# Gates and z: one 512-column matmul over high and low rows, halves added at eviction

## The chip, the cores and the metric

One core of one Trainium2 chip. The metric is the device time of one execution in microseconds (us), lowest is best; times of several runs are given as a median. A profile is one execution taken by the hardware profiler; its times count from its first instruction.

## The reference

Two layers over 256 latent tokens and 256 context tokens, 2048 channels, all in float32. Layer 0 projects the modulated, normalised tokens `h` by one weight `w_in` (2048 x 14400) into q, a gate, z, k, v, the X, B and C inputs of a state-space scan (SSD), and dt. Neighbourhood attention (16 heads of 128) is multiplied with the silu of the gate, the scan's output with the silu of z; both together go through `w_out`. Layer 1 is a gated short convolution.

```python
p = h @ w_in
...
ya = neighbourhood_attention(q, k, v, kc, vc, rpb).reshape(b, seq, NA_WIDTH)
ya = ya * jax.nn.silu(cols(p, COL_GATE_A, NA_WIDTH, 0))
...
yb = gated_group_rmsnorm(y_ssd + d * lat[0], cols(p, COL_Z, SSD_WIDTH, 0), ssm_norm_g)
out = jnp.concatenate([ya, yb], axis=-1) @ w_out
```

The gate, z, q and C are needed for the 256 latent tokens alone; k, v, X and B for latent and context tokens.

## The kernel before

**Precision.** Each float32 operand is split into a high part in the fast matmul format (`F32R`, a copy on ScalarE, called ACT) and a low part, the rest (a subtraction on VectorE, called DVE). A product is three matmuls into one PSUM bank: high by high, high by low, low by high. `hH[kb]` and `hL[kb]` (kb 0 to 15) are the split rows of block kb of the 2048 input channels, 512 columns each: 256 latent and 256 context tokens.

**Weights.** Loads of 512 KB (1024 elements on each of 128 partitions) come through the queue on SyncE in a written order (`q_proj`, `weight`), into five buffers `raw`; ACT writes the high half (L422) and DVE the low half (L429) into one of three places `w`. A load of a 512-column projection holds 2 row blocks in rows of 2 KB, one of a 256-column projection 4 row blocks in rows of 1 KB. Places used by the gate, z and C weights are shifted by 16 elements (`shifted`).

**Projections.** `proj(columns, kind, banks, ...)` walks the 16 row blocks and calls `chunk`, which takes the next split weight and issues matmuls (all recorded at L196). Kind "act" keeps the rows in the array and streams 512 weight columns (`mm_act`, for q, k, v). Kind 512 or 256 keeps a weight block of 128 columns in the array and streams 512 or 256 token columns (`mm_ws`): 512 for B and X, 256 for C, the gate and z. With 256, two weight blocks share a bank, 256 columns each, and three matmuls of 256 columns are issued for each weight block and row block.

**Order.** For group a (or s) 0 to 3, `do_qk`, `do_g` (gate, 512 columns), the values, and `do_ssd` (B, C, X in 4 banks, z with 512 columns) follow each other. Between the matmuls, `pump` lets generators issue their work: evictions (`urgent`), attention heads and scan groups (`side`), and dot products of the modulation for later (`back`). A planner keeps a time for each engine and each buffer and lets a task issue when its operands are due; `banks(n)` issues other work until n of the 8 PSUM banks are free; `reserve` keeps banks from side tasks toward the end of a projection.

**Eviction of gate and z** (`silu2_gen`): for each of the two banks of a unit, ACT takes a tanh of 512 columns (L1125) into a temporary, and DVE multiplies (th + 1) with the bank into `gt` or `sz` (L1127). It waits until the previous group is done with `gt` or `sz`, and until K of group 0 is done, since partial sums of K lie in those two buffers at the start.

**Tiles.** `xnT[kb]`, the transposed normalised rows, lie in the tiles of `hL` (blocks 0 and 1 in `Bl`, `Cl`) until block kb is modulated and split in `ada_gen`. Later the split mixer outputs (`mix`), the rows of layer 1 (`h1`) and its outputs (`y2`) take the places of `hH` and `hL`.

Of the kernel before, what the change touches and what calls it, by code (L numbers as in the profile page):

```python
# [9 lines left out]
F32R = mybir.dt.float32r  # L10
AF = mybir.ActivationFunctionType
ALU = mybir.AluOpType
# [129 lines left out]
def kernel(ctx: ExitStack, tc, x, cx, ada0, w0, adaT, w_in, w_out, sc_in, sc_out, rpb, small, const,  # L142
# [406 lines left out]
    for j in range(1, 8):  # L549
# [8 lines left out]
        if j < 7:  # L558
# [6 lines left out]
    order = list(range(0, 6)) + list(range(8, 16)) + [6, 7]  # L565
    ssd_cols = lambda s: [(w_in, COL_B + s * 256, 256), (w_in, COL_C + s * 256, 256), (w_in, COL_X + s * 512, 512),
                          (w_in, COL_Z + s * 512, 512)]
    q_proj(w_in, CG(0), 512)
# [4 lines left out]
    for a in range(1, 4):  # L573
        qk = [(w_in, CQ(a), 512), (w_in, CK(a), 512)]
        gv = [(w_in, CG(a), 512), (w_in, CV(a), 512)][::-1 if a in () else 1]
        for j_ in qk + gv + ssd_cols(a) if a < 3 else qk + ssd_cols(a) + gv:
            q_proj(*j_)
# [33 lines left out]
    xnT = [st([128, 512], ("Bl", "Cl")[kb] if kb < 2 else f"hL{kb}", name=f"xm{kb}") for kb in range(KB)]  # L611
# [51 lines left out]
    hH, hL = [None] * KB, [None] * KB  # L663

# [10 lines left out]
    def mm_ws(ps, actH, actL, H, Lo, n, first, last):  # L675

        for b in range(H.shape[-1] // 128):
            bb = slice(b * 128, (b + 1) * 128)
            if n == 512:
                o, f = ps[b], first  # L680
            else:
                o, f = ps[b // 2][:, (b % 2) * 256:(b % 2) * 256 + 256], first and b % 2 == 0
            mm(o, H[:, bb], actH[:, :n], f, False)
            mm(o, H[:, bb], actL[:, :n], False, False)
            mm(o, Lo[:, bb], actH[:, :n], False, last)
            if n == 512 or b % 2:
                pump()

    def chunk(kb0, kind, ps, first, last, lhs=None):
# [3 lines left out]
        for j in range(nb):  # L693
# [3 lines left out]
            if kind == "act":  # L697
                mm_act(ps, aH, aL, H[:, j], Lo[:, j], f, l)
            else:
                mm_ws(ps, aH, aL, H[:, j], Lo[:, j], kind, f, l)  # L700
# [21 lines left out]
    def ada_gen():  # L722
        bc = lambda ap: ap.unsqueeze(2).to_broadcast([128, 2, 2])
        for j in range(8):
# [39 lines left out]
            for ts in ((0, 1), (2,), (3,)) if j == 0 else ((0, 1, 2, 3),):  # L764
# [4 lines left out]
                for kb in (2 * j, 2 * j + 1):  # L769
# [5 lines left out]
                    if hH[kb] is None:  # L775
                        hH[kb] = st([128, 512], f"hH{kb}", F32R, name=f"hH{kb}")
# [13 lines left out]
                    if hL[kb] is None:  # L790
                        hL[kb] = st([128, 512], f"hL{kb}", F32R, name=f"hL{kb}")
# [213 lines left out]
    def put_mix(i, o):  # L1005
        if free_rows[0] > i % 16:

            yield W_("ACT", o)
            hl = st([128, 2, 256], f"hH{i}" if i < 16 else f"hL{i - 16}", F32R, name=f"mix{i}")
# [110 lines left out]
    def silu2_gen(key, a, ps, dst, ok):  # L1120
        yield when(lambda: ok())
        for b in range(2):
            yield W_("ACT", ps[b])
            th = tmp()
            E(S.activation(th, ps[b], AF.Tanh, scale=0.5))  # L1125
            yield W_("DVE", th)
# [1094 lines left out]
```

## Time and profile before

| | |
|---|---|
| median of 3 runs | 1740.03 us (1739.43 to 1740.67) |
| profiled execution, first to last instruction | 1738.3 us |
| TensorE (PE) busy | 1717.7 us, 99%, 9255 matmuls |
| weight loads (PEld) | 1451.5 us, 84% |
| VectorE (DVE) busy | 1253.3 us, 72% |
| ScalarE (ACT) busy | 776.2 us, 45% |
| memory read and written | 224 GB/s over the span |

The profiled execution has no time of its own beside its span; the median of the runs is 1.7 us over that span. Busy time of matmuls is modelled and overlaps from one to the next, so the distance between the starts of matmuls is what one takes in a stream. A row of the timeline is: start, length, engine, line and operation, output and inputs, shape, and how many instructions in a row were merged (x2). A row of a group is: line, engine, operation, output and inputs, shape, count, busy us, mean ns of one, and the idle time of the engine before them.

### The profile page before, as it was taken

Reading aid. Unit: us, or ns where it says so; the run is one execution under the profiler, and the core shown is the slowest. Engines: PE = TensorE matmul, PEld = TensorE weight load, DVE = VectorE, ACT = ScalarE, POOL = GpSimd, SP = SyncE. Lnnn points to the kernel's source line nnn. Section 1 sums busy time; section 2 is a strip of 40 time slices with the busy share of each in tenths; the row PEclk is TensorE's granted clock in tenths of the full one; section 3 lists DMA queues with packets and bytes.
Section 4 is the critical chain, followed back from the end, with each engine's and each line's share of the span. In section 5 each row is a group of like instructions: output and inputs, shape, how many; then the busy total and the mean of one; then the engine's idle time right before and its main releaser. Section 6 shows DMA issues by size and latency. Waiting matters only on the chain.

```text
span 1738.3 us, 24820 instructions
## 1 busy us (share of the span) xinstructions
PE 1717.7 (99%) x9255; PEld 1451.5 (84%) x9255; DVE 1253.3 (72%) x2108; ACT 776.2 (45%) x1367; POOL 33.2 (2%) x28
## 2 busy tenths in 40 slices
PE   6999999999999999999999999999999999999999
PEld 4777989889888889888888898888888888888887
DVE  5698787877576877676877687887668667665654
ACT  6434544445243445243435243665445344444442
POOL 0000100001000001000000000000000000000000
PEclk9999999999999999999999999999999999999999
DMA  9987644566754765755766567767867888776763
GB/s 375 366 319 271 206 135 142 180 209 187 228 183 151 234 210 183 227 188 164 230 221 195 191 196 248 258 225 254 280 204 260 267 272 284 246 241 191 248 213 114
DMA packets 192391, 391.03 MB, mean 225 GB/s; under 512 B 16200, under 2 KB 45960, under 8 KB 192016
## 3 DMA queue, kind: packets, MB, share of 16 engines
q1 hardware_dynamic: 184960, 382.88, 67.8%
q10 hardware_dynamic: 7312, 6.59, 1.2%
q8 instruction: 72, 1.18, 0.3%
q14 instruction: 47, 0.39, 0.1%
HBM read 379.79 MB, written 9.62 MB: 224 GB/s over the span
## 4 chain that ended last, share of the span: by engine, by line
PE 96%; DMA 2%; DVE 2%; issue 0%; SPq 0%; ACT 0%; POOL 0%; DVEq 0%; ACTq 0%
PE bank L196 93%; PE bank L200 3%; DMA raw<-in_ada 1%; DMA full<-dram_crow 1%; DVE csb L859 0%; DVE w L429 0%; DVE raw L859 0%; SPq L603 0%; DVE gt L818 0%; DVE yi L859 0%; DVE tmp L623 0%; DVE hL L792 0%; DVE sz L818 0%; DVE tmp L2116 0%; SPq L383 0%
## 5 line engine op out<-in xcount | busy, mean ns | idle before, releaser
L422 ACT CAST w<-raw 128x1024 fp32r<-128x1024 f32 (+1 forms) x344 | 359.8, 1047 | 554.7 <-PE bank L196 462.0
L429 DVE TENSOR_TENSOR w<-raw,w 128x1024 fp32r<-128x1024 f32 (+1 forms) x344 | 417.2, 1216 | 239.5 <-ACT w L422 238.2
L196 PE MATMUL bank<-hH,w 128*128 128x256 f32 (+1 forms) x2064 | 487.0, 325 | 0.0
L196 PE MATMUL bank<-w,hH 128*128 128x512 f32 x1280 | 405.7, 396 | 4.0 <-ACT hH L780 2.5
L196 PEld LDWEIGHTS bank<-hH,w 128*128 128x128 f32 x2064 | 345.3, 188 | 32.1 <-issue 1.7
L196 PE MATMUL bank<-hL,w 128*128 128x256 f32 (+1 forms) x1040 | 335.0, 322 | 0.0
L196 PEld LDWEIGHTS bank<-w,hH 128*128 128x128 f32 x1280 | 237.1, 188 | 56.3 <-DVE gt L818 3.4
L196 PE MATMUL bank<-w,hL 128*128 128x512 f32 x640 | 250.0, 391 | 0.2
L196 PEld LDWEIGHTS bank<-hL,w 128*128 128x128 f32 x1040 | 196.5, 189 | 14.5
L196 PE MATMUL bank<-w,h 128*128 128x512 f32 x768 | 178.2, 390 | 0.0
L196 PEld LDWEIGHTS bank<-w,h 128*128 128x128 f32 x768 | 144.1, 188 | 29.7
L888 DVE CUSTOM_DVE_ANT_0 raw<-raw,csb 128x1024 f32<-128x1024 f32 x128 | 155.3, 1218 | 11.9 <-DMA raw<-in_adaT 9.1
L196 PEld LDWEIGHTS bank<-w,hL 128*128 128x128 f32 x640 | 120.2, 188 | 25.7 <-DVE hL L792 0.9
L196 PE MATMUL bank<-w,mix 128*128 128x512 f32 x588 | 137.8, 391 | 0.0
L196 PEld LDWEIGHTS bank<-w,mix 128*128 128x128 f32 x588 | 109.7, 188 | 22.2 <-issue 0.3
L1371 DVE SCALAR_TENSOR_TENSOR tmp<-bank,cwh,tmp 128x508 f32<-128x508 f32 (+1 forms) x96 | 71.3, 746 | 1.9
L196 PE MATMUL bank<-KL,h 128*128 128x512 f32 x264 | 63.9, 390 | 0.0
L196 PEld LDWEIGHTS bank<-KL,h 128*128 128x128 f32 x264 | 49.5, 188 | 10.2
L196 PE MATMUL bank<-wH,h 128*128 128x512 f32 x168 | 55.7, 391 | 0.0
L196 PE MATMUL bank<-QT,h 128*128 128x512 f32 x168 | 55.7, 391 | 0.0
L429 DVE TENSOR_TENSOR wL<-raw,wH 128x1024 fp32r<-128x1024 f32 x31 | 37.9, 1223 | 23.9 <-ACT wH L422 23.8
L429 DVE TENSOR_TENSOR QL<-raw,QT 128x1024 fp32r<-128x1024 f32 x32 | 39.1, 1223 | 22.1 <-ACT QT L422 21.8
(306 smaller groups left out, 1962.3 us busy)
## 6 DMA issues: line engine op xcount, KB each, us to landing
raw<-in_w_in SPq DMA_DIRECT2D x196, 512.0 KB, 3.8
raw<-in_adaT SPq DMA_DIRECT2D x128, 512.0 KB, 4.8
raw<-in_sc_in SPq DMA_DIRECT2D x128, 512.0 KB, 4.7
raw<-in_w_out SPq DMA_DIRECT2D x64, 512.0 KB, 4.5
raw<-in_ada SPq DMA_DIRECT2D x35, 512.0 KB, 7.7
raw<-in_sc_out SPq DMA_DIRECT2D x32, 512.0 KB, 4.7
raw<-in_w SPq DMA_DIRECT2D x16, 512.0 KB, 5.5
tmp<-dram_csr SPq DMA_DIRECT2D x32, 256.0 KB, 5.2
```

What stands on the lines that cost most here:

```text
L196: E(T.matmul(o, l, r, start=start, stop=stop, skip_group_check=True))
L200: E(T.transpose(o, i, ident if k == 128 else ident[:k, :k]))
L422: E(S.copy(H, v))
L429: E(V.tensor_tensor(out=Lo, in0=v, in1=H.bitcast(F32), op=ALU.subtract))
L888: E(V.tensor_tensor_reduce(out=raw, in0=raw, in1=csb, scale=1.0, scalar=0.0, op0=ALU.mult, op1=ALU.add, accum_out=gp[:, h, m:m + 1]))
L1371: E(V.scalar_tensor_tensor(out=do, in0=di, scalar=cwh[:, 32 * k + ch:32 * k + ch + 1], in1=do, op0=ALU.mult, op1=ALU.add))
```

## The change

The 512 gate or z columns of a group are projected in two halves of 256 (two weight blocks each), with a bank for each weight block. For a weight block and a row block, one matmul of the high weights streams the 256 high and the 256 low latent columns side by side (512 columns, into the two halves of the bank), and a second streams the 256 high columns against the low weights into the first half. At the eviction ACT copies the bank's second half into `gt` or `sz`, DVE adds the first half to it, and, when both blocks of the half are there, tanh and the multiply follow from and to that buffer. The rows' high and low parts become one tile `hh[kb]` of two times 512 columns, so that one access pattern reaches both; the normalised rows of the start lie in the tiles of later odd blocks and in `Bl`, `Cl`. C keeps its three matmuls of 256 columns (`mm_quarter`). The weights of gate and z are loaded as 256-column projections.

```diff
@@ -563,16 +563,18 @@
...
     order = list(range(0, 6)) + list(range(8, 16)) + [6, 7]
+    halves = lambda c0: [(w_in, c0, 256), (w_in, c0 + 256, 256)]
     ssd_cols = lambda s: [(w_in, COL_B + s * 256, 256), (w_in, COL_C + s * 256, 256), (w_in, COL_X + s * 512, 512),
-                          (w_in, COL_Z + s * 512, 512)]
-    q_proj(w_in, CG(0), 512)
+                          *halves(COL_Z + s * 512)]
+    for j_ in halves(CG(0)):
+        q_proj(*j_)
     for r0 in (0, 1024):
...
         qk = [(w_in, CQ(a), 512), (w_in, CK(a), 512)]
-        gv = [(w_in, CG(a), 512), (w_in, CV(a), 512)][::-1 if a in () else 1]
+        gv = halves(CG(a)) + [(w_in, CV(a), 512)]
         for j_ in qk + gv + ssd_cols(a) if a < 3 else qk + ssd_cols(a) + gv:
@@ -608,7 +610,12 @@
...
     E(V.tensor_scalar(out=bs1, in0=P_("ab0")[:, 16:32], scalar1=1.0, scalar2=None, op0=ALU.add))
-    xnT = [st([128, 512], ("Bl", "Cl")[kb] if kb < 2 else f"hL{kb}", name=f"xm{kb}") for kb in range(KB)]
+    hh = [None] * KB
+    xnT = []
+    for j in range(7):
+        xm = st([128, 2, 512], f"h{2 * j + 3}", name=f"xm{j}")
+        xnT += [xm[:, 0], xm[:, 1]]
+    xnT += [st([128, 512], ("Bl", "Cl")[k], name=f"xm7{k}") for k in range(2)]
     rx = st([128, 4], "rx")
@@ -661,6 +668,7 @@
...
     hH, hL = [None] * KB, [None] * KB
+    row_of = lambda i: two((hH + hL)[i])
@@ -676,15 +684,28 @@
...
             bb = slice(b * 128, (b + 1) * 128)
-            if n == 512:
-                o, f = ps[b], first
-            else:
-                o, f = ps[b // 2][:, (b % 2) * 256:(b % 2) * 256 + 256], first and b % 2 == 0
-            mm(o, H[:, bb], actH[:, :n], f, False)
-            mm(o, H[:, bb], actL[:, :n], False, False)
-            mm(o, Lo[:, bb], actH[:, :n], False, last)
-            if n == 512 or b % 2:
-                pump()
+            mm(ps[b], H[:, bb], actH, first, False)
+            mm(ps[b], H[:, bb], actL, False, False)
+            mm(ps[b], Lo[:, bb], actH, False, last)
+            pump()
+
+    def mm_half(ps, rows_, H, Lo, first, last):
+
+        for b in range(2):
+            bb = slice(b * 128, (b + 1) * 128)
+            mm(two(ps[b]), H[:, bb], rows_[:, :, :256], first, False)
+            mm(ps[b][:, :256], Lo[:, bb], rows_[:, 0, :256], False, last)
+        pump()
+
+    def mm_quarter(ps, aH, aL, H, Lo, first, last):
+
+        for b in range(2):
+            bb = slice(b * 128, (b + 1) * 128)
+            o = ps[0][:, b * 256:b * 256 + 256]
+            mm(o, H[:, bb], aH[:, :256], first and b == 0, False)
+            mm(o, H[:, bb], aL[:, :256], False, False)
+            mm(o, Lo[:, bb], aH[:, :256], False, last)
+        pump()
@@ -696,8 +717,12 @@
...
                 mm_act(ps, aH, aL, H[:, j], Lo[:, j], f, l)
+            elif kind == 512:
+                mm_ws(ps, aH, aL, H[:, j], Lo[:, j], kind, f, l)
+            elif kind == 1:
+                mm_quarter(ps, aH, aL, H[:, j], Lo[:, j], f, l)
             else:
-                mm_ws(ps, aH, aL, H[:, j], Lo[:, j], kind, f, l)
+                mm_half(ps, hh[kb], H[:, j], Lo[:, j], f, l)
         used()
@@ -772,8 +797,9 @@
...
                     hf = tmp()
-                    if hH[kb] is None:
-                        hH[kb] = st([128, 512], f"hH{kb}", F32R, name=f"hH{kb}")
+                    if hh[kb] is None:
+                        hh[kb] = st([128, 2, 512], f"h{kb}", F32R)
+                        hH[kb], hL[kb] = hh[kb][:, 0], hh[kb][:, 1]
                     if ts == (0, 1):
@@ -787,8 +813,6 @@
...
                         yield W_("DVE", hf)
-                    if hL[kb] is None:
-                        hL[kb] = st([128, 512], f"hL{kb}", F32R, name=f"hL{kb}")
                     E(V.tensor_tensor(out=hL[kb][:, o], in0=hf[:, o], in1=hH[kb][:, o].bitcast(F32), op=ALU.subtract))
@@ -1006,7 +1030,7 @@
...
             yield W_("ACT", o)
-            hl = st([128, 2, 256], f"hH{i}" if i < 16 else f"hL{i - 16}", F32R, name=f"mix{i}")
+            hl = row_of(i)
             E(S.copy(hl[:, 0], o))
@@ -1117,18 +1141,24 @@
...
-    def silu2_gen(key, a, ps, dst, ok):
-        yield when(lambda: ok())
+    def silu2_gen(key, a, k, ps, dst, ok):
+        yield when(lambda: ok() and (k == 0 or (key, a, 0) in got))
+        o = dst[:, 2 * k:2 * k + 2, :].rearrange("p b c -> p (b c)")
         for b in range(2):
             yield W_("ACT", ps[b])
-            th = tmp()
-            E(S.activation(th, ps[b], AF.Tanh, scale=0.5))
-            yield W_("DVE", th)
-            E(V.scalar_tensor_tensor(out=dst[:, 2 * b:2 * b + 2, :].rearrange("p b c -> p (b c)"), in0=th, scalar=1.0,
-                                     in1=ps[b], op0=ALU.add, op1=ALU.mult))
-            give(free_t, th)
+            E(S.copy(dst[:, 2 * k + b, :], ps[b][:, 256:]))
+            yield W_("DVE", o)
+            E(V.tensor_tensor(out=dst[:, 2 * k + b, :], in0=ps[b][:, :256], in1=dst[:, 2 * k + b, :], op=ALU.add))
             give(free_b, ps[b])
-        got.add((key, a))
+        yield W_("ACT", o)
+        th = tmp()
+        E(S.activation(th, o, AF.Tanh, scale=0.5))
+        yield W_("DVE", th)
+        E(V.scalar_tensor_tensor(out=o, in0=th, scalar=1.0, in1=o, op0=ALU.add, op1=ALU.mult))
+        give(free_t, th)
+        got.add((key, a, k))
+        if k:
+            got.add((key, a))
@@ -1619,9 +1649,10 @@
...
     def do_g(a, nxt, leave=False):
-        psG = banks(2)
-        proj(512, 256, psG, nxt, leave)
-        spawn(urgent, silu2_gen("G", a, psG, gt, lambda: attn[0] >= 8 * a and (a or ("K", 0) in got)), 1)
+        for k in range(2):
+            psG = banks(2)
+            proj(256, 256, psG, nxt if k else 2, leave)
+            spawn(urgent, silu2_gen("G", a, k, psG, gt, lambda: attn[0] >= 8 * a and (a or ("K", 0) in got)), 1)
@@ -1629,15 +1660,16 @@
...
         psC, = banks(1)
-        proj(256, 256, [psC], 4)
+        proj(256, 1, [psC], 4)
         spawn(urgent, make_c(s, psC), 0, 2)
...
             spawn(urgent, make_x(s, gi, psX[2 * gi:2 * gi + 2]), 3)
-        psZ = banks(2)
-        proj(512, 256, psZ, nxt)
-        spawn(urgent, silu2_gen("Z", s, psZ, sz, lambda: ssd_done[0] >= 2 * s and ("K", 0) in got), 1)
+        for k in range(2):
+            psZ = banks(2)
+            proj(256, 256, psZ, nxt if k else 2)
+            spawn(urgent, silu2_gen("Z", s, k, psZ, sz, lambda: ssd_done[0] >= 2 * s and ("K", 0) in got), 1)
         for gi in range(2):
@@ -1701,7 +1733,7 @@
...
         for j, i in enumerate(pair):
-            hl = st([128, 2, 256], f"hH{i}" if i < 16 else f"hL{i - 16}", F32R, name=f"mix{i}")
+            hl = row_of(i)
             E(S.copy(hl[:, 0], m3[:, j]))
@@ -1843,7 +1875,7 @@
...
             if kb not in hls:
-                hls[kb] = st([128, 2, 256], f"hL{kb}", F32R, name=f"h1_{kb}")
+                hls[kb] = row_of(KB + kb)
                 h1[kb] = (hls[kb][:, 0], hls[kb][:, 1])
@@ -1971,8 +2003,6 @@
...
             turns = side[-1]
-            for kb in range(KB):
-                hH[kb] = hL[kb] = None
         passed.update(range(kcol, kcol + len(ns)))
@@ -2069,7 +2099,7 @@
...
                 yield W_("ACT", pt)
-                hl = st([128, 2, 256], f"hH{kb}", F32R, name=f"y2_{kb}")
+                hl = row_of(kb)
                 E(S.copy(hl[:, 0], p_))
...
```

## The prediction

> **What bounds the kernel.** I read the page first: span, engines, chain.
>
> ```profile
> span 1738.3 us, 24820 instructions
> PE 1717.7 (99%) x9255; PEld 1451.5 (84%) x9255; DVE 1253.3 (72%) x2108; ACT 776.2 (45%) x1367; POOL 33.2 (2%) x28
> PE 96%; DMA 2%; DVE 2%; issue 0%; SPq 0%; ACT 0%; POOL 0%; DVEq 0%; ACTq 0%
> ```
>
> TensorE is busy in 99% of the span and makes 96% of the chain that ended last. So the change can save only what it saves in TensorE's stream, and can lose only where it makes TensorE wait. The groups of matmuls, shapes apart, name the stream that is touched and one that already has the new form:
>
> ```profile
> L196 PE MATMUL bank<-hH,w 128*128 128x256 f32 x1280 | 234.1, 282 | 0.0
> L196 PE MATMUL bank<-hL,w 128*128 128x256 f32 x640 | 179.0, 280 | 0.0
> ```
>
> These 1920 matmuls of 256 columns are four gates, four z and four C projections. A gate or z unit has 4 weight blocks x 16 row blocks x 3 = 192, eight units 1536, in 512 triples; C keeps its 384. The mean of one (282 ns) overlaps its neighbours, so it is no price. The price is the distance between starts, which the timeline gives. Two stretches of the gates of group 1, each from one low-row matmul to the sixth after it (6 triples):
>
> ```profile
> 404.27 0.28 PE L196 MATMUL bank<-hL,w 128*128 128x256 f32 x1
> ...
> 406.39 0.28 PE L196 MATMUL bank<-hL,w 128*128 128x256 f32 x1
> ...
> 415.88 0.28 PE L196 MATMUL bank<-hL,w 128*128 128x256 f32 x1
> ...
> 417.92 0.28 PE L196 MATMUL bank<-hL,w 128*128 128x256 f32 x1
> ```
>
> 2.12/6 = 353 ns a triple (118 a matmul) in the first, 2.04/6 = 340 ns (113) in the second: the same work runs in two rhythms. How much of each there is, four units say (columns: stretch, length, PE busy and count, PEld, DVE, ACT, POOL, clock, DMA share, GB/s):
>
> ```profile
> 394.30:419.00 24.70, 24.70 (x214) 24.70 (x213) 20.41 (x40) 16.93 (x53) 4.50 (x2) 1.00 0.67 211
> 554.90:578.20 23.30, 23.30 (x200) 23.23 (x199) 21.88 (x29) 13.41 (x17) 0.00 (x0) 1.00 0.55 159
> 655.20:680.10 24.90, 24.90 (x225) 24.56 (x224) 18.06 (x30) 15.79 (x48) 2.90 (x1) 1.00 0.69 221
> 816.50:839.60 23.10, 23.10 (x201) 22.99 (x200) 22.20 (x31) 13.43 (x17) 0.00 (x0) 1.00 0.55 163
> ```
>
> Each holds 192 of the 256-column matmuls, and 22, 8, 33 and 9 others. Taking those out at about 0.1 us (some 2.4, 0.9, 2.9 and 0.9 us) leaves 116.1, 116.7, 114.6 and 115.6 ns for one: on average 115.8, a triple of 348. The clock is at its full 1.00, so the slow rhythm is not the clock.
>
> **What a 512-column matmul takes.** The X stage of group 0, just after a 256-column stage, from low row to low row:
>
> ```profile
> 235.19 0.40 PE L196 MATMUL bank<-hL,w 128*128 128x512 f32 x1
> 235.89 0.39 PE L196 MATMUL bank<-hL,w 128*128 128x512 f32 x1
> 236.58 0.39 PE L196 MATMUL bank<-hL,w 128*128 128x512 f32 x1
> ...
> 239.97 0.39 PE L196 MATMUL bank<-hL,w 128*128 128x512 f32 x1
> ```
>
> The first triples take 0.70 and 0.69 us (233 and 230 ns a matmul), and the five up to 239.97 take 3.39 us, 226 ns a matmul. That is exactly twice the 113 of the quick rhythm: a column costs 0.442 ns in either shape, and the merging by itself saves nothing against the quick rhythm. 512-column work starts slow too, but leaves the slow rhythm after some ten matmuls. 256-column work enters it at once, even out of a quick 512-column stage, and keeps it:
>
> ```profile
> 189.99 0.51 PE L196 MATMUL bank<-hH,w 128*128 128x512 f32 x2
> 190.33 0.28 PE L196 MATMUL bank<-hL,w 128*128 128x256 f32 x1
> ...
> 191.75 0.28 PE L196 MATMUL bank<-hL,w 128*128 128x256 f32 x1
> ```
>
> (1.42 us in 4 triples, 355.) The form that the change makes, a high block over two strided runs of 256 and a low block over 256, is in the trace in the attention's P.V, two pairs in a row:
>
> ```profile
> 283.53 0.39 PE L196 MATMUL bank<-P,VH 128*128 128x512 f32 x1
> 283.76 0.28 PE L196 MATMUL bank<-P,VL 128*128 128x256 f32 x1
> 283.88 0.39 PE L196 MATMUL bank<-P,VH 128*128 128x512 f32 x1
> 284.11 0.28 PE L196 MATMUL bank<-P,VL 128*128 128x256 f32 x1
> 284.23 0.31 PE L196 MATMUL bank<-P,VH 128*128 128x320 f32 x1
> ```
>
> Both pairs take 0.35 us, which is a triple's 348. But they are the first two after a change of work, where plain 512-column matmuls are slow as well, so they do not say what the twentieth pair takes.
>
> **The change part by part.** *Matmuls:* 512 triples become 512 pairs; 512 matmuls and weight loads go, the columns stay. If the pairs keep the quick rhythm throughout, one is 226 + 113 = 340 (rounded up, as the triples), 8 ns under the 348: 512 x 8 = 4.1 us gained. If they keep the slow one, a pair is 233 + 118 = 351, 3 ns over: 1.5 us lost. Those are the ends. I take the pairs to recover as the 512-column matmuls do, since two thirds of their columns come in that shape. What is left is the slow stretch after each interruption: I counted 35 places in the eight units where transposes or another task's matmuls break the run, and there are 16 starts of half units. At some 4 pairs of 10 ns, 51 breaks cost 2.0 us. The matmul term is -4.1 + 2.0 = -2.1 us.
>
> In the Trainium skill, "TensorE: Matmul & The Clock Gate", section "Back-to-back issue gap", a warm matmul costs its columns at 2.4 GHz and a fixed 2.5 ns. By that rule 512 matmuls fewer would save 512 x 2.5 = 1.3 us, an estimate; the trace, with 226 against 2 x 113, shows no such fixed part. The same page's "LDWEIGHTS (loading the stationary operand)" gives a load of 128 columns 128/1.2 = 107 ns, which would leave a 256-column matmul almost no margin and a 512-column one much; that would explain which shape recovers, and no row here proves it.
>
> *Eviction:* a unit had 2 tanh from PSUM and 2 multiplies; it gets 4 copies, 4 adds, 2 tanh and 2 multiplies from SBUF. Nearest rows (the P.V eviction has the same copy and add, the convolution the same tanh and multiply):
>
> ```profile
> L1255 DVE TENSOR_TENSOR half<-bank,half 128x256 f32<-128x256 f32 x16 | 6.8, 422 | 14.6 <-ACT half L1253 14.6
> L1253 ACT COPY half<-bank 128x256 f32<-128x256 f32 x16 | 6.0, 372 | 38.8 <-PE bank L196 38.8
> L1125 ACT ACTIVATE tmp<-bank 128x512 f32<-128x512 f32 x16 | 9.0, 596 | 6.1 <-DVE tmp L1378 6.1
> L1374 ACT ACTIVATE tmp<-tmp 128x512 f32<-128x512 f32 x24 | 15.1, 628 | 9.8 <-DVE tmp L1371 9.6
> L1127 DVE SCALAR_TENSOR_TENSOR sz<-tmp,bank 128x512 f32<-128x512 f32 x8 | 5.4, 684 | 0.4
> L1378 DVE SCALAR_TENSOR_TENSOR tmp<-tmp,tmp 128x512 f32<-128x512 f32 x24 | 16.4, 684 | 0.0
> ```
>
> DVE: 32 x 0.422 = +13.5 us, the multiply unchanged. ACT: 32 x 0.372 + 16 x 0.032 = +12.4 us. Per unit 1.7 and 1.6 us. Cover: ACT idles 6 us or more in each of the four stretches; DVE idles 4.3 and 6.8 us in the gate units, but only 1.4 and 0.9 us in the z units, where it still works off the convolutions of X. There the first half's two adds and one multiply (1.5 us) now fall inside the stage. I cost it at nothing, because a weight half that comes late is used only after the chunks already split ahead of it (three places of 2.9 us each); without that cover it is the second rival.
>
> *Banks:* each half takes 2 banks, a unit holds up to 4 for the time of an eviction. In most units the gates to gt and sz were open long before. In G(0) they open only when K(0) is done, so 2 (Q) + 2 (B) + 4 = 8 banks can be taken at once, and the K transposes must wait for Q's banks, whose last readers run late:
>
> ```profile
> 208.88 1.28 DVE L1059 TENSOR_TENSOR tmp<-bank,statq 128x512 f32<-128x512 f32 x2
> ```
>
> Between nothing (the matmuls of the second half run on) and about 3 us, the distance from the half's end to the second eviction of Q with its two steps; I take 0.1.
>
> *Loads:* 64 loads of 512 KB change from rows of 2 KB to rows of 1 KB, as B and C have. A stretch with mostly B and C rows (440 to 488 us) and one with mostly 2 KB rows (355 to 400 us):
>
> ```profile
> raw<-in_w_in SPq DMA_DIRECT2D x9, 512.0 KB, 3.6
> raw<-in_w_in SPq DMA_DIRECT2D x9, 512.0 KB, 3.7
> ```
>
> No difference to landing, and DMA is at 0.55 to 0.69 in the units: nothing. *Tiles:* high and low rows share one tile, the normalised rows of the start sit two blocks ahead in tiles that are written an iteration after their last reader: no new wait, nothing.
>
> Sum: -2.1 + 0.1 = -2.0 us against the span's 1738.3. The median of the runs, 1740.03, is 1.7 us over that span, and I carry this over: 1738.0.
>
> **Rivals.** *The pairs are quick at once* (each break costs next to nothing, since the 512-column member catches up within a pair): -4.1 + 0.1, 1736.0, and faster by 0.23%. For it speaks that 256-column runs turn quick by themselves after some interruptions (the row at 415.88); against it P.V's two slow pairs. Chance 0.30. *The half-boundary of z makes TensorE wait:* DVE runs its queue in order, the first half's adds wait for ACT's copies (2 x 0.372) in the stage where DVE idles only 0.9 to 1.4 us, and the low halves of the weights queue behind them. If all of a unit's 1.7 + 0.7 = 2.4 us lands on TensorE, four z units cost 9.7 us: 1738.0 + 9.7 = 1747.7. It decides (over 0.2%) from 1.4 us a unit, (3.5 + 2.0)/4. Against it: TensorE waits nowhere in these stretches now. Chance 0.14. *The pairs stay slow,* the change does not do what it might: +1.5, 1741.6, chance 0.10. *G(0) runs out of banks:* -2.0 + 3 = 1741.0, chance 0.08. The forecast keeps 0.38.
>
> **How the numbers follow.** A tenth of a per cent is about the spread of the three runs; 0.2% (3.5 us) is about what a measurement tells from no change. Faster: 0.30, and 0.05 of the forecast's 0.38 where breaks cost under 0.6 us: 0.35. Slower: the z rival's 0.14, and 0.02 of the G(0) case where it meets slow pairs: 0.16. Same: 0.49. The range reaches from the quick rival with 1 us of run spread, 1735.0, to slow pairs with part of the bank wait, 1743.0; it leaves out most of the z rival. The forecast's own range is 1736.5 to 1739.5.
>
> **What would show it.** Starts 226 and 113 apart in the middle of a unit confirm the recovery, 233 and 118 refute it; the first pairs after transposes give the price of a break. PE idle ended by the low halves (L429) in the z stretches, or a gap near 201 to 215 us, would make me wrong on the slow side; a gain over 5 us could not come from the matmuls at all, and would be another cause.

## The result: slower by 0.85%, and the profile after

The changed kernel takes 1755.32 us (median of 4 runs, 1752.28 to 1757.05) against 1739.77 us for the kernel before on the same chip: a ratio of 1.0085, interval 1.0071 to 1.0100. Forecast were 1738.0 us and a range up to 1743. The profiled run took 1752.28 us, the shortest of the four; its span is 1750.4, 12.1 us above the span before. From the page (span, engines, chain):

```profile
span 1750.4 us, 23840 instructions
PE 1721.5 (98%) x8743; PEld 1428.9 (82%) x8743; DVE 1263.8 (72%) x2140; ACT 786.6 (45%) x1399; POOL 35.1 (2%) x28
PE 94%; DMA 2%; DVE 2%; ACT 1%; issue 0%; SPq 0%; POOL 0%; DVEq 0%; ACTq 0%
```

512 matmuls are gone (9255 to 8743) and yet TensorE is busy 3.8 us *longer* (1717.7 to 1721.5), while its share falls to 98%: the work became dearer, and waits came besides. Below, G(1) is the gate unit of group 1, Z(0) the z unit of group 0, and the middle of a unit is the boundary between its two halves. DVE has 10.5 us more and ACT 10.4.

**The work.** Twelve pairs of a gate unit, undisturbed (a row of the windows: stretch, length, PE busy and count, PEld, DVE, ACT, POOL, clock, DMA share, GB/s):

```profile
416.30:420.53 4.23, 4.23 (x26) 3.67 (x25) 4.23 (x9) 2.39 (x4) 0.00 (x0) 1.00 0.19 64
```

24 matmuls start here (26 counts two still in flight): 4.23/12 = 353 ns a pair. In the starts of single matmuls it is 235 + 118, over and over; over all 512 of the merged matmuls the median is 235, and only 33 (6%) come at 229 or less. The pairs never recover. A triple took 348 before, on average over its two rhythms, so the merging costs some 512 x 5 ns = 2.6 us, an estimate.

**The waits.** What TensorE waited for (total, times, longest), without the rows that the kernel before has too:

```profile
PE bank L196 <- DVE tmp L1083: 3.4, 1, 3.4
PE bank L196 <- DVE w L429: 3.1, 2, 2.0
...
PE bank L196 <- DVE tmp L1401: 0.6, 1, 0.6
```

They sum to 7.1 us in four places. The largest is the middle of G(1); the timeline of PE, DVE and POOL there:

```profile
408.66 0.60 PE L196 MATMUL bank<-h,w 128*128 128x512 f32 x2
412.70 1.32 PE L196 MATMUL bank<-h,w 128*128 128x512 f32 x6 [3.45 <-DVE tmp L1083]
...
411.96 2.48 DVE L1083 TENSOR_TENSOR tmp<-bank,statk 128x512 f32<-128x512 f32 x4 [1.05 <-POOL statk L594]
...
408.12 3.80 POOL L594 TENSOR_TENSOR statk<-statk,const 128x16 f32<-128x16 f32 x1 [4.11 <-DVE statk L593]
```

The second half of the gates wants two banks, and the ones it gets are K's. K's rows leave them only when DVE normalises them (L1083), for which DVE needs the power of the sums that POOL (GpSimd) takes (L594, 3.80 us). The unit before took two banks once, and ran on through all of this. The second place is the middle of G(2), from 671.9 us. On DVE:

```profile
668.11 0.09 DVE L912 DVE_READ_ACCUMULATOR2_ANT gp<- 128x1 f32 x1
672.13 0.63 DVE L1178 TENSOR_TENSOR bias<-bias,const 128x128 f32<-128x128 f32 x3 [3.93 <-DMA bias<-in_rpb]
672.68 1.22 DVE L429 TENSOR_TENSOR w<-raw,w 128x1024 fp32r<-128x1024 f32 x1
```

DVE stands 3.93 us before an addition whose table has not landed; the low half of the next weights (L429) comes behind it in the queue, and TensorE waits 2.0 us for it. The other two are small: 1.13 us up to 1148.9 (again L429) and 0.59 in the middle of Z(0), for a bank that a convolution (L1401) still reads.

2.6 + 7.1 = 9.7 of the 12.1 us are found so. Set against the kernel before at equal counts of projected columns, the changed one is late by 0.8 us at 23 us (ahead of any changed unit: the wait for the first load, 11.2 us against 10.5, makes most of it), 2.5 at 400, 6.3 at 451, 6.6 at 650, 9.5 at 703, 10.4 at 1019 and 12.1 from 1201 to the end: the steps stand where the waits stand. What is left beside those 0.8, some 1.6 us, has no place of its own.

**A second price of a wait.** Of the four timed runs two have longer spans, 1754.6 and 1755.1 us, at a mean granted clock of 0.997. A later kernel (r4_after438 below) shows in its profile what that is. First it, then the changed kernel, each over the 3.4 us behind the same stall of G(1):

```profile
410.30:413.70 3.40, 3.27 (x12) 2.98 (x13) 3.28 (x8) 0.10 (x1) 0.00 (x0) 0.50 0.77 270
413.70:417.00 3.30, 3.30 (x25) 3.03 (x24) 2.78 (x6) 3.30 (x6) 0.00 (x0) 1.00 0.00 1
```

```profile
412.70:416.10 3.40, 3.40 (x25) 3.22 (x26) 3.40 (x8) 1.60 (x4) 0.00 (x0) 1.00 0.53 188
```

12 matmuls at clock 0.50 in the one, 25 at 1.00 in the other. After a wait TensorE may run at half clock for 3.4 us, which costs another 1.7 us; it does not come after each wait. 0.003 of 1755 us is three such stretches, about the difference between the spans; the fourth run (1751.9 us at 0.998) is 1.5 us longer where the same sum gives 3.5, so the mean clock is only a rough measure of it. The Trainium skill, "TensorE: Matmul & The Clock Gate", section "What's actually happening", states a free-running window of 3413 ns and half the rate after an idle one. The trace agrees with length and rate. It does not bear out that a whole window must be idle: in e7_unshift below a wait of 1.80 us was enough, and there the measurement decides.

### The profile page after: what moved, and what is told of

It reads as the page before. It is cut to its first block, busy times and chain, and to the rows that moved or that the text cites. A ratio compares the mean times of both kernels' runs of the same rounds, so it can differ in the third digit from the quotient of the medians.

```text
span 1750.4 us, 23840 instructions
## 1 busy us (share of the span) xinstructions
PE 1721.5 (98%) x8743; PEld 1428.9 (82%) x8743; DVE 1263.8 (72%) x2140; ACT 786.6 (45%) x1399; POOL 35.1 (2%) x28
## 4 chain that ended last, share of the span: by engine, by line
PE 94%; DMA 2%; DVE 2%; ACT 1%; issue 0%; SPq 0%; POOL 0%; DVEq 0%; ACTq 0%
PE bank L196 91%; PE bank L200 3%; DMA raw<-in_ada 1%; DMA full<-dram_crow 1%; DVE w L429 1%; DVE csb L883 0%; DMA tmp<-dram_csr 0%; DMA bias<-in_rpb 0%; DVE raw L883 0%; POOL statk L594 0%; ACT w L422 0%; SPq L605 0%; DVE gt L842 0%; SPq L383 0%; ACT tmp L1565 0%
## 5 line engine op out<-in xcount | busy, mean ns | idle before, releaser
L196 PE MATMUL bank<-w,h 128*128 128x512 f32 x3456 | 815.2, 392 | 5.6 <-ACT h L806 2.5
L196 PEld LDWEIGHTS bank<-w,h 128*128 128x128 f32 x3456 | 642.7, 188 | 143.6 <-DVE gt L842 3.5
L429 DVE TENSOR_TENSOR w<-raw,w 128x1024 fp32r<-128x1024 f32 (+1 forms) x344 | 416.7, 1215 | 237.7 <-ACT w L422 236.8
L196 PE MATMUL bank<-h,w 128*128 128x512 f32 (+1 forms) x2592 | 517.4, 356 | 6.1 <-DVE tmp L1083 3.4
L196 PEld LDWEIGHTS bank<-h,w 128*128 128x128 f32 x2592 | 422.9, 188 | 75.5 <-DVE tmp L1083 3.8
L196 PE MATMUL bank<-KL,h 128*128 128x512 f32 (+1 forms) x390 | 93.2, 386 | 0.5 <-DVE tmp L2146 0.5
L196 PE MATMUL bank<-QT,h 128*128 128x512 f32 (+1 forms) x260 | 85.3, 387 | 0.0
L196 PE MATMUL bank<-wH,h 128*128 128x512 f32 (+1 forms) x260 | 85.1, 386 | 0.0
L1401 DVE SCALAR_TENSOR_TENSOR tmp<-bank,cwh,tmp 128x508 f32<-128x508 f32 (+1 forms) x96 | 71.3, 745 | 1.9
L196 PEld LDWEIGHTS bank<-QT,h 128*128 128x128 f32 x260 | 48.8, 188 | 9.7
L429 DVE TENSOR_TENSOR QL<-raw,QT 128x1024 fp32r<-128x1024 f32 x32 | 39.1, 1222 | 22.5 <-ACT QT L422 22.1
L429 DVE TENSOR_TENSOR wL<-raw,wH 128x1024 fp32r<-128x1024 f32 x31 | 37.9, 1223 | 23.5 <-ACT wH L422 23.4
L429 DVE TENSOR_TENSOR KL<-raw,KL 128x1024 fp32r<-128x1024 f32 x32 | 39.1, 1223 | 18.3 <-ACT KL L422 18.1
L196 PE MATMUL bank<-QL,h 128*128 128x512 f32 (+1 forms) x130 | 50.2, 386 | 0.0
L196 PE MATMUL bank<-wL,h 128*128 128x512 f32 (+1 forms) x130 | 50.1, 386 | 0.0
```

Of the source, the lines that this page charges most:

```text
L196: E(T.matmul(o, l, r, start=start, stop=stop, skip_group_check=True))
L429: E(V.tensor_tensor(out=Lo, in0=v, in1=H.bitcast(F32), op=ALU.subtract))
L1401: E(V.scalar_tensor_tensor(out=do, in0=di, scalar=cwh[:, 32 * k + ch:32 * k + ch + 1], in1=do, op0=ALU.mult, op1=ALU.add))
```

## The experiments

Three questions: what sets the pairs' rhythm, which wait costs what, and whether the waits come from the half units or from the order of the work. Medians are in us; ratios are against the kernel before, run beside each (its medians 1740.06 to 1740.83).

### e1_split: the merged matmul in two

```diff
-            mm(two(ps[b]), H[:, bb], rows_[:, :, :256], first, False)
+            mm(ps[b][:, :256], H[:, bb], rows_[:, 0, :256], first, False)
+            mm(ps[b][:, 256:], H[:, bb], rows_[:, 1, :256], False, False)
```

> Everything of the changed kernel but the merged matmul: high by high and high by low are two matmuls of 256 columns into the two halves of the same bank. The profile of the changed kernel shows pairs of 235 + 118 = 353 ns against 348 ns a triple before, so the theory that the pairs keep the slow rhythm expects 512 x 5 = 2.6 us less than the changed kernel and the waits at the half boundaries unchanged: a span near 1748 us against 1750. If the merged matmul were a gain that something else hides, this kernel would be slower than the changed one.

1750.37 (1747.84 to 1751.32), ratio 1.0058 (1.0041 to 1.0075): 5 us come back where 2.6 were expected, and most of the loss stays, so the pairs' rhythm is the smaller part. The waits did not stay as they were, which the expectation took for granted: the one for K's banks is gone, and two others stand in the middles of G(1) and G(2):

```profile
PE bank L196 <- DVE w L429: 5.0, 2, 2.7
```

### e2_early_k: K's banks free early

ACT copies K's four banks out as soon as they are full; DVE normalises the copy.

```diff
...
+            if out_:
+                E(S.copy(jk, ps[t]))
+                give(free_b, ps[t])
...
```

> The changed kernel, but K of groups 1 to 3 gives its four banks back early: after a row block's squares ACT copies the bank to a temporary (some 0.6 us each, 12 copies), and DVE normalises there. Bank theory: the 3.45 us wait of TensorE at the half boundary of G(1) and the 2.0 us at G(2) go, the granted clock is 1.00 in every run, and the time falls from 1755 (span 1750) to about 1746 to 1748. Rival, that the 13.5 us of added DVE work and 12.4 us of ACT work are what costs: no faster than the changed kernel, since it adds 7 us to ACT.

1751.35 (1749.29 to 1751.84), ratio 1.0059 (1.0044 to 1.0074), and not the 1746 to 1748 that were expected. At G(1) 0.89 us of wait is left, for a low half; at G(2) it grew to 3.4. DVE there:

```profile
668.98 1.29 DVE L1188 TENSOR_TENSOR bias<-bias,const 128x128 f32<-128x128 f32 x6 [4.21 <-DMA bias<-in_rpb]
```

K's banks were the cause of the one wait. With it gone the kernel is some 4 us quicker, and the next cause stood behind it.

### e3_one_bank: half units without pairs

Half units, rows of 1 KB and joined tiles stay; the matmuls are triples into one bank for a half, with the old eviction.

```diff
...
-            psG = banks(2)
-            proj(256, 256, psG, nxt if k else 2, leave)
+            psG = banks(1)
+            proj(256, 1, psG, nxt if k else 1, leave)
...
```

> The half units, the loads in rows of 1 KB and the joined tiles of the changed kernel, but three matmuls of 256 columns with both weight blocks in one bank, and the eviction of before (one tanh and one multiply from the bank, no copy, no add). If the matmul form, the second bank and the longer eviction make the whole loss, this lies within 2 us of before, 1738 to 1742. If the loads, the tiles or the halving cost on their own, it stays at 1743 or above.

1744.43 (1742.90 to 1747.15), ratio 1.0023 (1.0013 to 1.0034): above the 1743 from which the expectation lays the loss on loads, tiles or halves. One large wait is left, 3.3 us up to 407.4 in the middle of G(1), with DVE standing until 403.8 for the bias table. At equal counts of projected columns the profile is late by 1.2 us at 130 (ahead of any half unit), 1.0 at 400, 4.0 at 420 and 4.3 at the end, so nearly all that the half units add comes with this wait. Without pairs and without extra banks there is still a stall.

### e4_contig: does the strided operand make the pairs slow?

The merged matmul streams 512 contiguous columns of the high rows, so the product with the low rows is left out.

```diff
-            mm(two(ps[b]), H[:, bb], rows_[:, :, :256], first, False)
+            mm(ps[b], H[:, bb], rows_[:, 0, :], first, False)
```

> The changed kernel with one access pattern altered: the merged matmul streams 512 columns in a row (high latent and high context columns) in place of two runs of 256; the product with the low latent rows is left out. If the strided reading keeps the pairs slow, starts are 227 and 113 apart in most of a unit and about 6 us go; if it is the change of shape from one matmul to the next, they stay at 235 and 118 and the time at that of the changed kernel.

1752.96 in one run; starts are again 235 and 118 ns apart. The two separate runs of 256 columns are not the reason for the rhythm.

### e5_early_late, e6_one_bank_late: the bias addition held back

e2 and e3, with the addition put off by 8 us of planned TensorE time (the planner's own clock, when it lays down the order) after its DMA was issued:

```diff
...
+        if hd < 12:
+            t0_ = plan.t["PE"]
+            yield when(lambda: plan.t["PE"] > t0_ + 8000)
         yield W_("DVE", bt)
...
```

> As changed, with two edits that take waits away: K's four banks are copied out by ACT as soon as they are full, and the addition of the bias table on DVE is held back until 8 us of planned TensorE time have gone by since its DMA was issued. Theory (the loss is stalls at the half boundaries, because the second half needs two more banks at a moment when DVE is held up): the stalls of 3.4 us in G(1) and 2.0 us in G(2) and the one of 0.8 us in Z(0) go, no stretch of clock 0.5 follows them, and what stays is the rhythm of the pairs (512 x 5 ns = 2.6 us), about 1.2 us at 1147 and about 1 us at the start: 1744 to 1746 us. Rival (DVE's added 13.5 us and ACT's 12.4 us are the load that lasts, whatever the banks): it stays at 1750 or more, and other waits take the place of those removed.

> As e3_one_bank (half units, 1 KB loads, joined tiles, triples in one bank) with the bias addition held back by 8 us of planned TensorE time. Theory: the one stall of 3.4 us at 403.8 was DVE standing behind the bias table's DMA; it goes, and the time is that of the kernel before, 1739 to 1742 us. Rival (halves, loads or joined tiles cost something on their own): it stays at 1744.

Both expectations failed. e5: 1754.23 (1752.54 to 1754.93), ratio 1.0079 (1.0064 to 1.0094); e6: 1744.11 (1742.92 to 1747.17), ratio 1.0023 (1.0014 to 1.0033). TensorE waits again in the middles of G(1) and G(2), 1.8 and 4.1 us in e5, 2.4 and 0.2 in e6. The DMA of the bias table (issued on SyncE) and DVE in e5:

```profile
402.94 0.42 DVE L1617 TENSOR_TENSOR half<-bank,yi 128x256 f32<-128x256 f32 x1 [4.51 <-PE bank L196]
...
663.88 1.25 SPq L1183 DMA_DIRECT2D bias<-in_rpb  x2
...
670.57 1.25 DVE L1191 TENSOR_TENSOR bias<-bias,const 128x128 f32<-128x128 f32 x6 [4.71 <-DMA bias<-in_rpb]
```

and in e6:

```profile
403.57 0.87 DVE L1635 SCALAR_TENSOR_TENSOR half<-half,small,bank 128x256 f32<-128x256 f32 x2 [3.99 <-PE bank L200]
405.58 3.49 DVE L429 TENSOR_TENSOR w<-raw,w 128x1024 fp32r<-128x1024 f32 x3
```

At 403 us a different instruction now holds DVE for as long: one that waits for a result of TensorE, which has projections to do as well. At G(1), then, my first theory, that the bias table is the cause, fell. At G(2) it was not tested: DVE stood at the addition from 665.9, only 2 us after the DMA was issued at 663.88, since the planned 8 us are not 8 us on the chip, and the table was there at 670.5. What the stalls share is that DVE stands some 4 us in the middle of G(1) or G(2) and comes back with up to three low halves due at once.

### e7_unshift, e8_group: what keeps the pairs slow

```diff
-            if w is w_in and (COL_G <= c0 < COL_K or COL_C <= c0 < COL_DT):
+            if w is w_in and COL_C <= c0 < COL_DT:
```

> As e5_early_late, but the gate and z weights are not shifted by 16 columns in the chunk that is split. If the pairs' rhythm of 235 + 118 ns hangs on where the weight block begins, the pairs here run at 226 + 113 and the time falls by 512 x 14 ns = 7 us against e5; if it hangs on the alternation of lengths, the pairs stay at 353 ns and the time is that of e5 within 1 us.

```diff
         for b in range(2):
-            bb = slice(b * 128, (b + 1) * 128)
-            mm(two(ps[b]), H[:, bb], rows_[:, :, :256], first, False)
-            mm(ps[b][:, :256], Lo[:, bb], rows_[:, 0, :256], False, last)
+            mm(two(ps[b]), H[:, b * 128:(b + 1) * 128], rows_[:, :, :256], first, False)
+        for b in range(2):
+            mm(ps[b][:, :256], Lo[:, b * 128:(b + 1) * 128], rows_[:, 0, :256], False, last)
```

> As e5_early_late, with the four matmuls of a row block in the order high, high, low, low (two of 512 columns, then two of 256). If each change of length keeps the slow rhythm up, halving the changes lets a part recover: 702 down to some 690 ns for a row block, or 1 to 3 us less than e5. If the rhythm is set once by the start of the unit, no change.

e7: 1752.96 (two runs, ratio 1.0073, 1.0053 to 1.0093). Two pairs take 693 to 711 ns, on average 702 against e5's 706: where the weights begin matters a little (some starts are 113 there, others 241), and does not bring 680. e8: 1748.09 (1748.08 to 1749.18), ratio 1.0046 (1.0030 to 1.0062), 6 us under e5 where 1 to 3 were expected. A row block settles at 693 ns: 226 + 236 + 118 + 113, and the mean of the undisturbed ones is 695. So of two equal matmuls in a row one is quick, and in alternation, with the weights placed as in the change, none is. The rhythm gives 256 x 13 ns = 3.3 of the 6 us; the waits moved as well. Two triples take 696: the best arrangement of the merged form tried here gains 1 to 3 ns on them. What makes the rhythm stays open.

### p1_price430, p2_price438: the kernel before in another order

The planner orders the work by its own prices. Here only its price of a matmul moves by 1%; every instruction stays as it was in the kernel before.

```diff
-                return 9 + 0.434 * n, 190
+                return 9 + 0.430 * n, 190
```

> The kernel before with one number of its planner changed: the price of an F32R matmul is 9 + 0.430 n ns in place of 9 + 0.434 n. Every instruction stays, only their order on the engines shifts. Theory A (the stretches after K of passes 1 and 2, near 404 and 670 us, have no slack: ACT is in K's sums of squares, DVE stands in order behind a TensorE result or the bias table, and the three split chunks just last in the order before): another order of the same work loses 2 to 5 us there, 1742 to 1746 us. Rival B (the stalls belong to the half units: their second set of banks and their eviction): no stall, 1739 to 1741 us.

> The kernel before with the planner's price of an F32R matmul at 9 + 0.438 n ns. Theory A (no slack near 404 and 670 us): a stall of 1 us or more at one of them, 1741 to 1746 us. Rival B (half units alone cause the stalls): 1739 to 1741 us.

p1: 1745.11 (1742.81 to 1745.89), ratio 1.0028 (1.0017 to 1.0039). p2: 1743.12 (1741.71 to 1745.07), ratio 1.0019 (1.0009 to 1.0028). The kernel before has no such waits in its own order; p1 has

```profile
PE bank L196 <- DVE hL L792: 2.5, 2, 1.5
...
PE bank L196 <- DVE w L429: 1.3, 1, 1.3
PE bank L200 <- DVE tmp L1059: 1.2, 2, 0.9
```

(the first at 133 to 137, where the kernel before waits 1.2 us at 145 to 147 for another tile; the second up to 1140.9; the third at 417, where K's normalised rows are late), and p2 waits 0.8 us at 404 and as long at 1138. DVE in p2 at 404, the low half behind the bias table, as in the changed kernel:

```profile
403.36 0.63 DVE L1148 TENSOR_TENSOR bias<-bias,const 128x128 f32<-128x128 f32 x3 [0.95 <-DMA bias<-in_rpb]
403.91 1.22 DVE L429 TENSOR_TENSOR w<-raw,w 128x1024 fp32r<-128x1024 f32 x1
```

Rival B falls: the old instructions, without any half unit, lose 3 to 5 us in another order, as much as e3 and e6 lose in all. Theory A has the time right and the places only in part. Set against the kernel before at equal counts of projected columns, p1 is late by 0.3 us at 400, 2.4 at 440, 2.6 at 1110 and 5.0 at the end, p2 by 1.2 at 440, 1.1 at 1110 and 2.1 at the end: about half of each loss comes near 404, none at 670, and half at 1139, which the theory did not name; p2's 0.8 us at 404 is less than the 1 us expected. So the stretch behind K of pass 1 has little slack, it is not the only one, and the kernel before has an order in which none of these waits arises.

### q1_group and q2_whole: the change, grouped; and without halves

q1 is the changed kernel with e8's order of matmuls and nothing else. q2 takes whole units in four banks, with four high and then four low blocks, and K's banks early.

> The changed kernel with the four matmuls of a row block in the order high, high, low, low, and nothing else. From e8 a row block takes 693 ns so (226 + 236 + 118 + 113) against 706 for two alternating pairs: 256 blocks x 13 ns = 3.3 us less than the change from the rhythm alone. The stalls of G(1) and G(2) stay within their few us: 1747 to 1753 us. If Theory A holds, the stalls move by more than that, since the planner sees the same prices but other ends of chunks.

> Whole units of 512 columns in four banks (2 KB weight rows, no half boundary at all), in each row block four matmuls of 512 columns, then four of 256; K's banks copied out early as in e2. If the half boundary makes the stalls (rival B), there is none at 404 and 670, the rhythm is that of e8 or better (693 ns per half block or less), and the time is 1738 to 1742 us. If the stretches after K have no slack whatever the units (theory A), stalls of several us stay there: 1744 to 1752 us.

q1: 1745.07 (1742.83 to 1746.63, without one run of 3550.09 us that its clock of 1.000 does not explain), ratio 1.0030 (1.0018 to 1.0041): 10 us less than the changed kernel, by splitting one loop of two lines in two. Some 3 of them are the rhythm, shown by these 12 high and 12 low blocks (24 starts in 4.16 us, 347 ns a pair against 353):

```profile
410.50:414.66 4.16, 4.16 (x26) 3.65 (x25) 2.00 (x3) 2.41 (x5) 2.13 (x1) 1.00 0.78 305
```

The other 7 are more than the rhythm can explain, and the time lies under the 1747 to 1753 that the rhythm alone was expected to give. The waits moved, as theory A has it: G(1) has no wait for K's banks any more, and two are left, in G(2) and Z(0):

```profile
PE bank L196 <- DVE w L429: 1.5, 1, 1.5
...
PE bank L196 <- DVE tmp L1401: 1.3, 1, 1.3
```

q2: 1749.29 (1748.79 to 1750.13), ratio 1.0054 (1.0039 to 1.0069). There is no wait at 404 or 670 us, as rival B has it, but the time is theory A's: new waits, most of them for banks, stand at 312, 680, 1029 and 1132. Neither reading is right as it was put, and four banks for a unit are no way out.

### r1 to r4, s1, s2: each kernel in several orders

The planner's horizon says how far an engine's planned time may run ahead of TensorE's when a task issues its next work. r1 is q1 with the horizon for urgent work at 4.0 in place of 4.5 us; r2 is q1 with the side horizon at 2.2 and the bias addition held back; r3 and r4 are the changed kernel, s1 and s2 the grouped one, at the prices of p1 and p2.

> q1_group with the planner's horizon for urgent work at 4.0 in place of 4.5 us. If the stalls left in q1_group (1.3 us in Z(0), 1.5 us in G(2)) go with the order of work, they move: 1739 to 1748 us, one of the two gone or another in its place. If they belong to the half boundary's second set of banks, both stay where they are, and the time is 1744 to 1746 us.

> q1_group with the planner's horizon for side work at 2.2 in place of 2.5 us and the bias addition held back as in e5. As r1: other stalls if they go with the order (1739 to 1748 us), the same two if they belong to the half boundary (1744 to 1746 us).

> The changed kernel with the planner's price of an F32R matmul at 9 + 0.430 n ns. Pairs keep 235 + 118 ns. If the stalls belong to the half boundaries: G(1) and G(2) again 3.4 and 2.0 us, 1753 to 1757 us. If they go with the order: the places change and the time moves by 3 us or more either way, between 1744 and 1760 us.

> The changed kernel with the price at 9 + 0.438 n ns. The same two readings as r3_after430: 1753 to 1757 us with the stalls at G(1) and G(2) if they belong to the half boundaries, a time that moves by 3 us or more if they go with the order. In no order below 1743 us, since the pairs' rhythm costs 2.6 us.

> q1_group with the planner's price of an F32R matmul at 9 + 0.430 n ns. If the rhythm is all that grouping changes, it takes 3.3 us less than r3_after430 (1746.6): 1743 to 1744 us. If the order decides, any time from 1740 to 1750 us, with a stall of 1 us or more that r3_after430 does not have, or without one that it has.

> q1_group with the price at 9 + 0.438 n ns. If the rhythm is all that grouping changes, 3.3 us less than r4_after438 (1751.2): 1747 to 1749 us. If the order decides, any time from 1740 to 1752 us, with stalls in other places than in r4_after438 (406.9 and 671.5).

| planner's price | kernel before | changed kernel | changed, grouped |
|---|---|---|---|
| 0.434 | 1 | 1755.32, 1.0085 (1.0071 to 1.0100) | 1745.07, 1.0030 (1.0018 to 1.0041) |
| 0.430 | 1745.11, 1.0028 (1.0017 to 1.0039) | 1746.62, 1.0036 (1.0023 to 1.0050) | 1753.13, 1.0069 (1.0054 to 1.0084) |
| 0.438 | 1743.12, 1.0019 (1.0009 to 1.0028) | 1751.17, 1.0067 (1.0049 to 1.0085) | 1748.35, 1.0039 (1.0024 to 1.0053) |

r1: 1742.19 (1740.85 to 1743.36), ratio 1.0010 (1.0001 to 1.0020). r2: 1743.91 (1741.46 to 1747.38), ratio 1.0021 (1.0011 to 1.0030); its wait in Z(0) is gone, the one in G(2) stays (2.1 us, again behind the bias table), and half of each reading holds.

The same instructions move by up to 8.7 us (1755.32 to 1746.62) with the order, pairs at 353 ns in each. r1 and r3 came out as the order reading had it. s1 lies far above the 1744 that the rhythm alone would give, and above the 1750 that the order reading allowed. r4 is between the readings (it has the waits of G(1) and G(2), and is 4 us quicker all the same). s2 came out as the rhythm reading had it: 2.8 us under r4, with waits in the same two places. Where the waits are, in r4 and s2 (first r4):

```profile
PE bank L196 <- DVE tmp L1083: 3.1, 1, 3.1
...
PE bank L196 <- DVE w L429: 2.4, 2, 2.0
```

```profile
PE bank L196 <- DVE tmp L1083: 2.4, 1, 2.4
PE bank L196 <- DVE w L429: 1.7, 2, 1.1
```

In s1 a convolution is late (4.4 us at 504, where none of the others waits), and 6.8 us at half clock follow. In r1 nothing is left in any half boundary, only a low half at 1138:

```profile
PE bank L196 <- DVE w L429: 1.6, 2, 1.3
```

The wait for K's banks in the middle of G(1) is in the changed kernel, r4 and s2, and in none of the three orders of the kernel before: that one the half units bring with them, where the order does not happen to hide it. Over the three prices the changed kernel is 8 us slower than the kernel before (0.63% against 0.16%), and grouping takes 3 us off it (0.46%). That is as much as the rhythm, but at the three prices one by one grouping takes 10 off, adds 6.5 and takes 3 off, so the agreement may be chance. And the change itself costs 14.8 us at one price, 1.5 at another: three orders are too few to say what it costs in a fair order. That stays open.

No version beats the kernel before. r1, the nearest, is within 0.2% of it.

## Why the prediction was wrong

The forecast saw a span 2.0 us shorter, and the profile's is 12.1 us longer. Of these 14.1 us the matmul term makes 4.7, the banks 3.4, late low halves 3.1, a bank that a convolution still reads 0.6, and 2.4 have no term (0.8 of them at the start). The median of the runs lies 3 us over the profiled one, about what two stretches at half clock cost. So the waits, which the prediction put at 0.1 us, are the larger part.

*Matmul term, -2.1 us: measured +2.6.* The step that failed is "I take the pairs to recover as the 512-column matmuls do". The prediction had the ends right (quick pairs gain, slow pairs lose) and even the two slow P.V pairs; it chose against the nearest rows because plain 512-column matmuls recover. Those follow their own kind; a pair alternates, and in the change alternation holds 235 + 118 to the end. The rival "pairs stay slow" was right in mechanism, and 2 ns a pair too low. The statement that merging saves nothing against the quick rhythm held: the quickest 512-column starts are 226 ns apart, twice 113, and even grouped a row block takes 693 ns, not 680.

*Eviction at nothing: 3.1 us of waits for low halves came.* Its own instructions came out as priced,

```profile
L1149 ACT COPY sz<-bank x16: 356/372/394, 303.1 to 1041.0; 128x256 f32<-128x256 f32 x16
```

```profile
L1151 DVE TENSOR_TENSOR sz<-bank,sz x16: 410/414/417, 305.1 to 1042.8; 128x256 f32<-128x256 f32 x16
```

(shortest, median and longest in ns), against 372 and 422. The cover is what failed: "a weight half that comes late is used only after the chunks already split ahead of it (three places of 2.9 us each)". Those places are a reserve of up to 8.7 us only if they are full. In the middle of G(2) DVE stood 3.93 us on the bias table, and the reserve was gone. Whether DVE's added work led to this or the order alone is not shown. The z rival had this mechanism (DVE in order, low halves behind) and the wrong stage: it gave z 9.7 us, where TensorE waited 0.6; the gates had the banks and the table against them.

*Banks, +0.1 us: measured 3.45 at G(1).* The step looked at G(0) alone and said that "in most units the gates to gt and sz were open long before". G(0) has no wait, close to what was said. But the second pair of banks depends not on the gate to gt but on who else holds banks, and after K that is K, with four.

*Loads and tiles at nothing:* not tried apart. e3 has both, and of the 4.3 us of its span 1.2 are there ahead of any half unit (0.2 in e6, with the same tiles) and 3.0 come with the one wait at G(1); r1 has both and ends at a ratio of 1.0010. So no cost of their own shows, but no run parts them from the order of the work.

*Not foreseen at all:* that the order is itself worth 3 to 9 us. The prediction took the planner's order as given and priced only instructions, and its range of 8 us is no wider than what a change of 1% in one price does to the changed kernel (8.7 us). And a wait can cost 1.7 us more through the clock. The size of the miss is in part the luck of one order: at the price of 0.430 the changed kernel takes 1746.62 us, still outside the range.

## What to carry to other kernels

Where one engine is busy 99% of the time, ask first what the change does to the order of work beside it: shift one price of the scheduler in the old kernel and see how far its time moves, since that spread belongs in every forecast. Price a new mix of shapes by the mix, not by the members, when starts depend on the neighbour. And when a unit begins to take its buffers in two steps, list who holds buffers at the second step.

## What the runs showed of the hardware

With distinct weights for each, matmuls of 512 and 256 columns start 226 and 113 ns apart at best; in strict alternation they stay at 235 and 118 at clock 1.00, for contiguous and strided operands alike (e4), and with the weights 16 columns elsewhere (e7) at 232 to 241 and 113 to 120; two of a kind in a row take 226 + 236 or 118 + 113 (e8, q1). A wait of TensorE of 1.8 to 4.4 us can be followed by 3.4 us at half clock. e7 has such a stretch behind a wait of 1.8 us (12 matmuls at 0.51, where the next 3.4 us hold 22):

```profile
408.90:412.30 3.40, 3.40 (x12) 2.82 (x12) 3.33 (x7) 0.72 (x2) 1.79 (x1) 0.51 0.98 336
412.50:415.90 3.40, 3.40 (x22) 2.97 (x21) 2.04 (x3) 1.99 (x4) 0.91 (x1) 1.00 0.68 246
```

while the changed kernel's wait of 3.45 us was followed by none in its profile. In e4, which has the same waits in the same places, the one of 3.3 us at G(1) was followed by one.
